# Convolutional FFN of a two-layer model: weight scales by exponent shifts out of PSUM, and one pool of four raw weight tiles

## The chip, the cores and the metric

The kernel runs on one core of a Trainium2 chip. The metric is the device time of one execution in microseconds (us). TensorE does matrix products into PSUM; VectorE, ScalarE and GpSimd do elementwise work, GpSimd only in SBUF; SyncE issues the transfers (DMAs) in one in-order queue.

## The reference

A model of two layers, 1024 tokens, width 1024, in float32. Layer 0 has a hybrid attention, layer 1 a latent attention (neither is touched here); after each comes the same kind of FFN:

```python
def conv_ffn(h, w_up, conv_w, conv_b, w_down):      # FFN_DIM = 2816, CONV_WIDTH = 3
    u = h @ w_up                                     # 1024 -> 2 * 2816
    u = causal_depthwise_conv(u, conv_w) + conv_b    # 3 taps along the tokens, per channel
    g, val = jnp.split(u, 2, axis=-1)
    return (jax.nn.silu(g) * val) @ w_down           # 2816 -> 1024

for i in range(2):
    x = x + mixer_i(rms_norm(x, attn_norm[i]))
    x = x + conv_ffn(rms_norm(x, ffn_norm[i]), ffn_w_up[i], ffn_conv_w[i], ffn_conv_b[i], ffn_w_down[i])
return rms_norm(x, final_norm)
```

## The kernel before

Every product is done in split precision: an operand is a high and a low 16-bit float (`up_h`, `up_l`; `dn_h`, `dn_l`; `qah`, `qal`), and three products of the halves are added in PSUM. So that the halves fit the range of the 16-bit format, each weight tile and each group of activations is first multiplied by a power of two, and the result is later multiplied by its inverse. Finding these powers of two is what the change is about.

**Stages of one FFN.** `mixer_out` (line 786) opens the pools, finds the scale of the norm's gain (`sh`, inverse `ish`), prepares the first two up weight tiles and runs the second half of the attention's output projection (`op.second`), after each block of which the block is normalised (`norm_xn`) and turned into seven blocks for a Strassen-like product (`block_turn`). `ffn_body` (line 812) then loops over j = 0..21. `ffn_up(j)` multiplies 12 x 7 times with the weights of tile j (`product`, line 561), evacuates the products into `u` (`keep` on ScalarE, line 567; `plus` on VectorE, line 571), asks for the weights of tile j + 2 (`up_weights`), and does the convolution (lines 603 to 606), SiLU, gating (line 610) and a Square that sums the squares of the gated values (line 611). Some j also ask for the down weights of a pair of tiles (`down_weights`, 11 in one FFN). When a group of one or two pairs is complete, `ffn_down` finds the group's scale (`down_scale`) and multiplies (line 722), adding into `x` (line 728) on VectorE.

**One up weight tile** (`up_weights`, line 461): two loads of 512 KB into two raw tiles (tag `up_raw`, two buffers, so one set); a Square of each on ScalarE that also gives the sums per partition, `ss` (line 470); VectorE adds the two sums into `sb` (line 473); TensorE multiplies with a matrix of ones, which spreads the sum over all partitions (line 476); VectorE scales it out of PSUM into `t` (line 478). `power` (line 451) then takes t to the power -1/2 on GpSimd (line 455), masks the mantissa away on VectorE, which gives the scale `s` (line 336), and three more VectorE instructions give the inverse `u` (reciprocal, times 1.25, mask). VectorE multiplies the tile's convolution weights `cw` by `u` and `ish` (line 483). GpSimd makes three sums of the raw tiles (lines 495 to 500), and ScalarE and VectorE or GpSimd split them (lines 636 to 640). **One down tile** (`down_weights`, line 642) goes the same way, with its own set of two raw tiles (tag `dn_raw`, which the gain and every other normalised block use too) and one more product on GpSimd, `uu` (line 664). `down_scale` (line 689) adds the sums of squares of a group, spreads them, takes the larger of its pairs (line 699) and calls `power`.

**Order.** Nothing is ordered by hand. A planner orders each engine's instructions when the program is built, from estimated durations, the order in which the code asks for them and the raised priorities (`tc.high_priority`); a buffer of a tag is given to the next tile when its last reader is done. On the chip each engine and the load queue then run strictly in that order, so an instruction that waits holds up all that stand behind it.

Of the kernel before, what the change touches and what calls it, by code (L numbers as in the profile page):

```python
# [21 lines left out]
P = 128  # L22
S = 1024
D = 1024
# [22 lines left out]
def model_kernel(ctx: ExitStack, tc: tile.TileContext, a: dict, out: bass.AP, dbg: dict):  # L47
# [58 lines left out]
    nc.gpsimd.memset(ones_sq, 1.0)  # L106
# [354 lines left out]
    def up_weights(li, j, up, cw, ish):  # L461
# [4 lines left out]
        ss = up.tile([P, 2], F32, name="wss", tag="wss", bufs=2)  # L466
        for q in range(2):
            raw.append(up.tile([P, 4, 256], F32, name="up_raw", tag="up_raw", bufs=2))
            load = nc.sync.dma_start(out=raw[q], in_=a["w_up"][li, j, :, q * 4:q * 4 + 4, :])
            nc.scalar.activation(out=sums.rearrange("p k t c -> p k (t c)"), in_=raw[q],  # L470
                                 func=AF.Square, accum_out=ss[:, q:q + 1])
# [79 lines left out]
    def ffn_up(li, j, up, dns, pairs, blocks, cw, weights, ish):  # L551
# [45 lines left out]
        if j + 2 < NF:  # L597
            weights.append(up_weights(li, j + 2, up, cw, ish))
# [12 lines left out]
        nc.scalar.activation(out=gate, in_=val, func=AF.Square, accum_out=pair["ss"][:, h:h + 1])  # L611
# [11 lines left out]
    def new_pair(q, dns):  # L623
        dn = dns[q % 2]
        g = [g for g in GROUPS if q in g][0]
        if q == g[0]:
            grp[0] = {"ss": dns[0].tile([P, len(g), 2], F32, name="gss", tag="gss", bufs=2),
                      "u": dns[0].tile([P, len(g), 1], F32, name="dnu", tag="dnu", bufs=2),
                      "uu": dns[0].tile([P, len(g), 1], F32, name="duu", tag="duu", bufs=2)}
        group = grp[0]  # L630
        return {"g": dn.tile([P, 2, S], F32, name="g", tag="g", bufs=1 + q % 2), "dn": dn, "q": q,
                **{k: group[k][:, g.index(q)] for k in ("ss", "u", "uu")}, "group": group}
# [9 lines left out]
    def down_weights(li, up, pair, weights):  # L642
# [3 lines left out]
        for j in (2 * q, 2 * q + 1):  # L646
            raw.append(up.tile([P, D], F32, name="dn_raw", tag="dn_raw", bufs=2))
            nc.sync.dma_start(out=raw[-1], in_=a["ffn_w_down"][li, j * P:(j + 1) * P, :])
        sums = up.tile([P, 2, 512], F32, name="dn_s", tag="up_s", bufs=SB)
        ss = up.tile([P, 2], F32, name="dss", tag="wss", bufs=2)  # L650
        for i in range(2):
            nc.scalar.activation(out=sums.rearrange("p a c -> p (a c)"), in_=raw[i], func=AF.Square,
                                 accum_out=ss[:, i:i + 1])
        sb = up.tile([P, 2], BF16, name="dsb", tag="wsb", bufs=2)
        nc.vector.tensor_tensor(out=sb, in0=ss[:, 0:1].broadcast_to([P, 2]),
                                in1=ss[:, 1:2].broadcast_to([P, 2]), op=ALU.add)
        st = bank("sb", 1)
        nc.tensor.matmul(st[:, :2], ones_sq, sb, start=True, stop=True)
        t = up.tile([P, 1], F32, name="dt", tag="wt", bufs=2)
        nc.vector.tensor_scalar(out=t, in0=st[:, :1], scalar1=1.05 * 2.0 ** -28, scalar2=1e-30,  # L660
                                op0=ALU.mult, op1=ALU.max)
# [27 lines left out]
    def down_scale(ps_, dn, bank_=None):  # L689
# [3 lines left out]
        with tc.high_priority(TP):  # L693
# [928 lines left out]
```

## Time and profile before

| what | value |
|---|---|
| median of 3 runs | 2531.49 us (2531.34 to 2533.38) |
| the profiled execution | 2533.1 us, of which the span from first to last instruction is 2531.3 |
| busy in the span: TensorE / VectorE / ScalarE / GpSimd | 2286.3 / 2013.6 / 1516.3 / 1251.4 us |
| mean granted TensorE clock | 0.966 |
| first FFN body | about 627 to 1300 us |
| second FFN body | about 1830 to 2506 us |

The trace has one row for each instruction; views group them. In the rows below PE is TensorE, PEld its weight loads, DVE VectorE, ACT ScalarE, POOL GpSimd, SPq the load queue; L473 is line 473 of the kernel; `out<-in` are the names of tiles. "A <- B: total, times, longest" means that engine and line A stood idle until B was done. A busy TensorE is not TensorE at its peak, as matmuls overlap.

### The profile page before, as it was taken

What the parts mean: (1) busy time and instruction counts of PE and PEld (TensorE: products, weight loads), DVE (VectorE), ACT (ScalarE), POOL (GpSimd) and SP (SyncE); (2) the same over time, 40 slices, a digit from 0 to 9 for tenths busy, and PEclk for the clock granted to TensorE, in tenths of its full rate; (3) what the DMA queues carried; (4) which work ended last, traced back from release to release, by engine and by line L of the source; (5) the groups of instructions that cost most, each with busy time, mean ns of one, the idle gap of its engine ahead of it and who ended that gap; (6) DMA issues with size and microseconds to landing.
All of it is one profiled execution on the core that took longest, in us unless ns stands there. A gap on an engine that the chain in (4) does not pass through costs nothing. (4 is left out here: it accounts for less than half of the span.)

```text
span 2531.3 us, 32238 instructions
## 1 busy us (share of the span) xinstructions
PE 2286.3 (90%) x10960; PEld 1358.3 (54%) x10960; DVE 2013.6 (80%) x3577; ACT 1516.3 (60%) x2533; POOL 1251.4 (49%) x1312
## 2 busy tenths in 40 slices
PE   8999999998889989898999877878898998989898
PEld 7877778676333434343448665556643343434343
DVE  6777887768787887887886887885878788788787
ACT  5676666536665555656545777773666556555653
POOL 4444433206465564656316777640746556465631
PEclk9999999899999999999999898989899999999999
DMA  4466633661111111111131787899121111111111
GB/s 134 101 138 121 127 77 80 201 178 61 61 55 50 45 56 50 50 42 59 34 112 32 141 169 150 161 257 242 51 63 52 49 48 53 50 50 42 59 42 67
DMA packets 324549, 228.46 MB, mean 90 GB/s; under 512 B 280288, under 2 KB 283360, under 8 KB 323936
## 3 DMA queue, kind: packets, MB, share of 16 engines
q1 hardware_dynamic: 324384, 226.40, 34.9%
q8 instruction: 86, 1.41, 0.2%
q14 instruction: 79, 0.65, 0.1%
HBM read 127.79 MB, written 25.43 MB: 61 GB/s over the span
## 5 line engine op out<-in xcount | busy, mean ns | idle before, releaser
L561 PEld LDWEIGHTS <-up_h 128*128 128x128 f16 x2464 | 241.6, 99 | 364.2 <-issue 73.8
L264 ACT ACTIVATE prob<-prob,m 128x512 f32<-128x512 f32 (+7 forms) x256 | 198.5, 776 | 103.7 <-DVE m L261 81.5
L289 DVE SCALAR_TENSOR_TENSOR hl<-prob,rl,hl 128x128 f16<-128x128 f32 (+6 forms) x196 | 199.0, 1027 | 25.5 <-ACT hl L288 24.6
L561 PEld LDWEIGHTS <-up_l 128*128 128x128 f16 x1232 | 122.2, 99 | 170.6 <-DVE up_l L640 21.7
L125 PE MATMUL bank_t<-hw_h,hTh 128*128 128x384 f32 x512 | 186.1, 366 | 2.8 <-DVE hTl L110 1.6
L126 PE MATMUL bank_t<-hw_l,hTh 128*128 128x384 f32 x512 | 176.9, 345 | 1.7 <-DVE hw_l L110 1.7
L288 ACT ACTIVATE hl<-prob,rl 128x128 f16<-128x128 f32 (+6 forms) x196 | 149.0, 778 | 47.6 <-DVE prob L1025 17.1
L127 PE MATMUL bank_t<-hw_h,hTl 128*128 128x384 f32 x512 | 175.4, 343 | 0.4 <-DVE hTl L110 0.4
L252 PE MATMUL wide<-k,q 96*128 96x512 f32 (+7 forms) x576 | 142.1, 388 | 37.1 <-DVE m L261 28.8
L261 DVE CUSTOM_DVE_ANT_0 prob<-wide,maskc 128x256 f32<-128x256 f32 (+3 forms) x192 | 143.9, 751 | 36.0 <-PE wide L252 32.9
L722 PEld LDWEIGHTS <-qah 128*128 128x128 f16 x896 | 86.3, 98 | 115.1 <-issue 10.7
L470 ACT ACTIVATE up_s<-up_raw 128x1024 f32<-128x1024 f32 x88 | 92.7, 1053 | 88.8 <-DMA up_raw<-in_w_up_dram 70.1
L728 DVE SCALAR_TENSOR_TENSOR x<-bank_a,gun,x 128x512 f32<-128x512 f32 x168 | 123.2, 743 | 19.3 <-PE bank_a L722 17.9
L252 PEld LDWEIGHTS wide<-k,q 128*128 128x128 f32 (+1 forms) x576 | 106.5, 214 | 57.1 <-DVE m L261 34.9
L500 POOL TENSOR_TENSOR up_raw<-up_raw,up_s 128x512 f32<-128x512 f32 x44 | 81.3, 1848 | 100.4 <-DVE up_l L640 69.0
L495 POOL TENSOR_TENSOR up_s<-up_raw 128x512 f32<-128x512 f32 x44 | 59.1, 1343 | 134.5 <-ACT up_s L470 128.3
L640 DVE SCALAR_TENSOR_TENSOR up_l<-up_raw,wsc,up_h 128x1024 f16<-128x1024 f32 x84 | 119.1, 1426 | 0.9 <-ACT up_h L639 0.7
L728 DVE SCALAR_TENSOR_TENSOR x<-bank_b,gun,x 128x512 f32<-128x512 f32 x152 | 112.5, 742 | 7.3 <-PE bank_b L722 7.1
L639 ACT ACTIVATE up_h<-up_raw,wsc 128x1024 f16<-128x1024 f32 x84 | 92.2, 1141 | 42.6 <-DVE wsc L336 42.5
L329 PEld LDWEIGHTS <-V 128*128 128x128 f16 x840 | 74.6, 100 | 73.6 <-issue 28.5
L110 POOL TENSOR_TENSOR up_l<-up_raw,up_h 128x512 f16<-128x512 f32 (+1 forms) x48 | 72.9, 1518 | 74.3 <-ACT up_h L117 44.3
L125 PEld LDWEIGHTS bank_t<-hw_h,hTh 128*128 128x128 f32 x512 | 97.5, 191 | 19.1 <-issue 12.3
(457 smaller groups left out, 7425.5 us busy)
## 6 DMA issues: line engine op xcount, KB each, us to landing
up_raw<-in_w_up_dram SPq DMA_DIRECT2D x88, 512.0 KB, 3.8
dn_raw<-in_ffn_w_down_dram SPq DMA_DIRECT2D x44, 512.0 KB, 3.7
hw_raw<-in_w_hyb_dram SPq DMA_DIRECT2D x32, 384.0 KB, 3.7
OTa<-ohl SPq DMA_DIRECT2D x16, 512.0 KB, 2.9
oa<-OTa SPq DMA_DIRECT2D x16, 512.0 KB, 6.2
OTb<-ohl SPq DMA_DIRECT2D x16, 512.0 KB, 3.8
xb<-in_x_dram SPq DMA_DIRECT2D x8, 512.0 KB, 5.7
x<-in_x_dram SPq DMA_DIRECT2D x8, 512.0 KB, 7.2
```

Source lines behind the costliest of these rows:

```text
L125: nc.tensor.matmul(out_, sh, mh, start=start, stop=False)
L126: nc.tensor.matmul(out_, sh, ml, start=False, stop=False)
L127: nc.tensor.matmul(out_, sl, mh, start=False, stop=stop)
L252: nc.tensor.matmul(sp[:, h * 512:h * 512 + w], q[:, qs], k[:, c:c + w], start=n == 0, stop=n == len(passes) - 1)
L261: nc.vector.tensor_tensor_reduce(out=pv, in0=sv, in1=mv, scale=-scale, scalar=3e38, op0=ALU.add, op1=ALU.min, accum_out=m)
L264: nc.scalar.activation(out=pv, in_=pv, func=AF.Exp, bias=m, scale=-1.0, accum_out=l)
L288: nc.scalar.activation(out=hi, in_=v, func=AF.Copy, scale=r)
L289: nc.vector.scalar_tensor_tensor(out=lo, in0=v, scalar=r, in1=hi, op0=ALU.mult, op1=ALU.subtract)
L470: nc.scalar.activation(out=sums.rearrange("p k t c -> p k (t c)"), in_=raw[q], func=AF.Square, accum_out=ss[:, q:q + 1])
L561: nc.tensor.matmul(o, w[side][p][:, k], blocks[block][q][:, k], start=first and k == n == 0, stop=k == 3 and n == 2, skip_group_check=not ...
L640: nc.vector.scalar_tensor_tensor(out=l, in0=x, scalar=s, in1=h, op0=ALU.mult, op1=ALU.subtract)
L728: nc.vector.scalar_tensor_tensor(out=x_, in0=m, scalar=un, in1=x_, op0=ALU.mult, op1=ALU.add)
```

## The change

The scale is no longer a power -1/2 with a masked mantissa: the exponent of the sum is halved by shifts and subtracted from a constant, as integers. The constant factor that `t` had goes into the matrix of ones, whose entries become 1.0625 x 2^-28. The sums of halves go: the Square writes its sums as bfloat16, and TensorE adds the two columns itself, as two matmuls into the same place. The inverse `u` is one integer addition, and VectorE's product of the convolution weights becomes a ScalarE Copy with scale `u`, while `ish` is multiplied into all of them at once on GpSimd. `down_scale` finds its scale in the same way, and `uu` goes. Raw tiles of up and down weights, the gain and every other normalised block share one tag, `raw`, of four buffers. The second up tile is asked for after the output projection's second half.

```diff
-    nc.gpsimd.memset(ones_sq, 1.0)
+    nc.gpsimd.memset(ones_sq, 1.0625 * 2.0 ** -28)
...
+    def halved(x, t):
+        nc.vector.tensor_scalar(out=x, in0=t.bitcast(I32), scalar1=24, scalar2=23,
+                                op0=ALU.logical_shift_right, op1=ALU.logical_shift_left)
+
     def power(s, u, t, pool):
-        v = pool.tile([P, 1], F32, name="pw", tag="pw", bufs=2)
+        x = pool.tile([P, 1], I32, name="pw", tag="pw", bufs=2)
         with tc.high_priority(TP):
-            nc.gpsimd.tensor_tensor(out=v, in0=t, in1=neghalf[:, :1], op=ALU.pow)
-            pow2(s, v)
-        nc.vector.reciprocal(out=v, in_=s)
-        nc.vector.tensor_scalar(out=v, in0=v, scalar1=1.25, scalar2=None, op0=ALU.mult)
-        pow2(u, v)
+            halved(x, t)
+            nc.vector.tensor_scalar(out=s.bitcast(I32), in0=x, scalar1=-1, scalar2=189 << 23,
+                                    op0=ALU.mult, op1=ALU.add)
+        nc.vector.tensor_scalar(out=u.bitcast(I32), in0=x, scalar1=65 << 23, scalar2=None, op0=ALU.add)
+
+    def over_partitions(st, sums):
+        for n, c in enumerate(sums):
+            nc.tensor.matmul(st, ones_sq, c, start=n == 0, stop=n == len(sums) - 1)
...
-        ss = up.tile([P, 2], F32, name="wss", tag="wss", bufs=2)
+        ss = up.tile([P, 2], BF16, name="wss", tag="wss", bufs=2)
...
-            raw.append(up.tile([P, 4, 256], F32, name="up_raw", tag="up_raw", bufs=2))
+            raw.append(up.tile([P, 4, 256], F32, name="up_raw", tag="raw", bufs=4))
...
-        sb = up.tile([P, 2], BF16, name="wsb", tag="wsb", bufs=2)
-        nc.vector.tensor_tensor(out=sb, in0=ss[:, 0:1].broadcast_to([P, 2]),
-                                in1=ss[:, 1:2].broadcast_to([P, 2]), op=ALU.add)
         st = bank("sb", 1)
-        nc.tensor.matmul(st[:, :2], ones_sq, sb, start=True, stop=True)
-        t = up.tile([P, 1], F32, name="wt", tag="wt", bufs=2)
-        nc.vector.tensor_scalar(out=t, in0=st[:, :1], scalar1=1.05 * 2.0 ** -28, scalar2=1e-30,
-                                op0=ALU.mult, op1=ALU.max)
+        over_partitions(st[:, :2], [ss[:, q:q + 1].broadcast_to([P, 2]) for q in range(2)])
...
-        power(s, u, t, up)
-        nc.vector.tensor_scalar(out=cw[:, j, :, 0:3], in0=cw[:, j, :, 0:3], scalar1=u, scalar2=ish,
-                                op0=ALU.mult, op1=ALU.mult)
+        power(s, u, st[:, :1], up)
+        nc.scalar.activation(out=cw[:, j, :, 0:3], in_=cw[:, j, :, 0:3], func=AF.Copy, scale=u)
...
-        power(s, pair["u"], t, up)
-        nc.gpsimd.tensor_scalar(out=pair["uu"], in0=pair["u"], scalar1=pair["u"], scalar2=1.05 * 2.0 ** -28,
-                                op0=ALU.mult, op1=ALU.mult)
+        power(s, pair["u"], st[:, :1], up)
...
-            sb = dn.tile([P, np_], BF16, name="gsb", tag="gsb", bufs=2)
-            nc.vector.tensor_tensor(out=sb, in0=ss[:, :, 0], in1=ss[:, :, 1], op=ALU.add)
-            st = (bank_ or bank_b)()
-            nc.tensor.matmul(st[:, :np_], ones_sq, sb, start=True, stop=True)
-            y, t = (dn.tile([P, n], F32, name=f"gy{n}", tag=f"gy{n}", bufs=2) for n in (2, 1))
-            nc.vector.tensor_tensor_reduce(out=y[:, :np_], in0=st[:, :np_], in1=grp_["uu"][:, :, 0], scale=1.0,
-                                           scalar=1e-30, op0=ALU.mult, op1=ALU.max, accum_out=t)
...
-        power(tau, un, t, dn)
...
+            over_partitions(st[:, :2], ss)
+            halved(r.bitcast(I32), st[:, :np_])
+            nc.vector.tensor_scalar(out=r.bitcast(I32), in0=r.bitcast(I32), scalar1=65 << 23, scalar2=None, op0=ALU.add)
+            nc.vector.tensor_scalar(out=un, in0=r[:, 0:1], scalar1=gu[:, 0:1], scalar2=None, op0=ALU.mult)
+            if np_ == 2:
+                nc.vector.tensor_scalar(out=un, in0=r[:, 1:2], scalar1=gu[:, 1:2], scalar2=un, op0=ALU.mult, op1=ALU.max)
+            nc.vector.tensor_scalar(out=tau.bitcast(I32), in0=un.bitcast(I32), scalar1=-1, scalar2=254 << 23,
+                                    op0=ALU.mult, op1=ALU.add)
             nc.vector.tensor_scalar(out=sg, in0=gu, scalar1=tau, scalar2=None, op0=ALU.mult)
...
-        gain = load_gain(up, f"ffn_norm{li}", D, "dn_raw", 2)
+        gain = load_gain(up, f"ffn_norm{li}", D, "raw", 4)
...
-        weights = [up_weights(li, j, up, cw, ish) for j in range(2)]
+        nc.gpsimd.tensor_scalar(out=cw[:, :, :, 0:3], in0=cw[:, :, :, 0:3], scalar1=ish, scalar2=1.0,
+                                op0=ALU.mult, op1=ALU.mult)
+        weights = [up_weights(li, 0, up, cw)]
...
-            xn = norm_xn(up, op.x[b], gain, *(("acc", AB), ("dn_raw", 2))[SO.index(b) % 2])
+            xn = norm_xn(up, op.x[b], gain, *(("acc", AB), ("raw", 4))[SO.index(b) % 2])
...
         op.second(nxt)
+        weights.append(up_weights(li, 1, up, cw))
```

## Rows read from the trace of the kernel before

**Rows 1.** Stages (length; busy PE, PEld, DVE, ACT, POOL): step, first body, both.

```profile
561.00:620.00 59.00, 55.41 (x249) 43.00 (x247) 45.74 (x70) 32.56 (x53) 35.48 (x33) 0.97 0.29 99
...
627.00:1300.00 673.00, 612.92 (x2766) 268.70 (x2763) 547.34 (x776) 391.00 (x555) 347.06 (x318) 0.98 0.16 51
...
sum 1349.00, PE 1231.62 PEld 539.38 DVE 1095.95 ACT 782.49 POOL 694.00; mean PE 615.81 PEld 269.69 DVE 547.98 ACT 391.24 POOL 347.00
```

**Rows 2.** TensorE's waits in the first FFN body (us in total, times, longest).

```profile
PE prod L561 <- ACT u L567: 11.1, 8, 3.2
PE prod L561 <- ACT up_h L639: 8.2, 6, 4.2
PE prod L561 <- DVE u L571: 6.8, 8, 3.3
PE bank_b L722 <- DVE x L728: 6.8, 9, 1.8
PE prod L561 <- DVE up_l L640: 6.6, 5, 2.4
PE sb L476 <- DVE wsb L473: 3.7, 5, 1.0
PE bank_b L697 <- DVE gsb L695: 3.4, 3, 2.2
...
PE sb L658 <- DVE wt L478: 2.2, 1, 2.2
```

**Rows 3.** Waits of all engines over the whole span.

```profile
ACT up_s L470 <- DMA up_raw<-in_w_up_dram: 70.1, 37, 5.9
...
ACT up_h L639 <- DVE wsc L336: 42.5, 20, 3.6
```

**Rows 4.** Groups of VectorE, whole span: busy us, mean ns, idle us before.

```profile
L640 DVE SCALAR_TENSOR_TENSOR up_l<-up_raw,wsc,up_h 128x1024 f16<-128x1024 f32 x84 | 119.1, 1426 | 0.9 <-ACT up_h L639 0.7
...
L483 DVE TENSOR_SCALAR convw<-convw,wun,hun 128x6 f32<-128x6 f32 x44 | 27.2, 618 | 0.5
...
L473 DVE TENSOR_TENSOR wsb<-wss 128x2 bf16<-128x2 f32 x44 | 18.8, 426 | 36.6 <-ACT up_s L470 36.5
...
L458 DVE TENSOR_SCALAR pw<-pw 128x1 f32<-128x1 f32 x82 | 12.2, 148 | 1.2
...
L336 DVE TENSOR_SCALAR wsc<-pw 128x1 int32<-128x1 int32 x44 | 6.6, 149 | 16.4 <-POOL pw L455 16.2
L478 DVE TENSOR_SCALAR wt<-sb 128x1 f32<-128x1 f32 x44 | 6.4, 146 | 0.0
...
L695 DVE TENSOR_TENSOR gsb<-gss 128x2 bf16<-128x2 f32 (+1 forms) x14 | 4.8, 344 | 5.5 <-ACT acc L611 5.5
```

**Rows 5.** Two tiles' instructions: duration ns as min/median/max, then first and last start.

```profile
L483 DVE TENSOR_SCALAR convw<-convw,wun,hun x44: 274/370/2118, 587.4 to 2449.0; 128x6 f32<-128x6 f32 x44
...
L336 DVE TENSOR_SCALAR wsc<-pw x44: 134/153/155, 581.7 to 2445.7; 128x1 int32<-128x1 int32 x44
```

**Rows 6.** Groups of GpSimd, whole span.

```profile
L455 POOL TENSOR_TENSOR pw<-wt,neghalf 128x1 f32<-128x1 f32 x44 | 43.5, 988 | 45.3 <-DVE wt L478 45.3
...
L664 POOL TENSOR_SCALAR duu<-dnu 128x1 f32<-128x1 f32 x22 | 13.3, 605 | 22.2 <-DVE dnu L336 17.9 <-ACT qah L639 3.7
...
L455 POOL TENSOR_TENSOR pw<-gy,neghalf 128x1 f32<-128x1 f32 x14 | 11.9, 848 | 90.5 <-DVE gy L699 90.5
```

**Rows 7.** Groups: small ScalarE instruction, sum matmul. Timeline: four sum matmuls in attention.

```profile
L969 ACT ACTIVATE lams<-lams 128x2 f32<-128x2 f32 x1 | 0.2, 191 | 0.0
...
L476 PE MATMUL sb<-wsb,ones_sq 128*128 128x2 bf16 x44 | 7.5, 171 | 10.5 <-DVE wsb L473 9.3 <-DVE dnu L336 1.2
...
66.92 0.25 PE L883 MATMUL bank_t<-g,wsq 128*128 128x2 bf16 x4
```

**Rows 8.** Timeline of VectorE, 1020 to 1024 us: start, us, instruction.

```profile
1020.96 0.15 DVE L478 TENSOR_SCALAR wt<-sb 128x1 f32<-128x1 f32 x1
...
1023.18 0.15 DVE L336 TENSOR_SCALAR wsc<-pw 128x1 int32<-128x1 int32 x1 [0.44 <-POOL pw L455]
```

More of the change, by code (lines that the diff above doesn't have):

```diff
@@ L464, in up_weights @@
+    def up_weights(li, j, up, cw):
         raw = []
         sums = up.tile([P, 4, 2, P], F32, name="up_s", tag="up_s", bufs=SB)
[L466 removed]
+        ss = up.tile([P, 2], BF16, name="wss", tag="wss", bufs=2)
         for q in range(2):
[L468 removed]
+            raw.append(up.tile([P, 4, 256], F32, name="up_raw", tag="raw", bufs=4))
             load = nc.sync.dma_start(out=raw[q], in_=a["w_up"][li, j, :, q * 4:q * 4 + 4, :])
[L470 to L471 removed]
@@ L472, in up_weights @@
-        sb = up.tile([P, 2], BF16, name="wsb", tag="wsb", bufs=2)
-        nc.vector.tensor_tensor(out=sb, in0=ss[:, 0:1].broadcast_to([P, 2]),
-                                in1=ss[:, 1:2].broadcast_to([P, 2]), op=ALU.add)
+            with nc.allow_low_precision("it chooses a power of two"):
+                nc.scalar.activation(out=sums.rearrange("p k t c -> p k (t c)"), in_=raw[q],
+                                     func=AF.Square, accum_out=ss[:, q:q + 1])
         st = bank("sb", 1)
-        nc.tensor.matmul(st[:, :2], ones_sq, sb, start=True, stop=True)
@@ L549, in block_turn, with ffn_up @@
         put(blocks, "t4", tok, t4)
-    def ffn_up(li, j, up, dns, pairs, blocks, cw, weights, ish):
+    def ffn_up(li, j, up, dns, pairs, blocks, cw, weights):
         w, _ = weights.pop(0)
@@ L597, in ffn_up @@
         if j + 2 < NF:
-            weights.append(up_weights(li, j + 2, up, cw, ish))
+            weights.append(up_weights(li, j + 2, up, cw))
         gate = up.tile([P, S], F32, name="acc", tag="acc", bufs=AB)
@@ L610, in ffn_up @@
         nc.vector.tensor_tensor(out=val, in0=gate, in1=val, op=ALU.mult)
-        nc.scalar.activation(out=gate, in_=val, func=AF.Square, accum_out=pair["ss"][:, h:h + 1])
+        with nc.allow_low_precision("it chooses a power of two"):
+            nc.scalar.activation(out=gate, in_=val, func=AF.Square, accum_out=pair["ss"][:, h:h + 1])
     GROUPS = ((0,), (1, 2), (3, 4), (5, 6), (7, 8), (9,), (10,))
@@ L626, in new_pair @@
         if q == g[0]:
-            grp[0] = {"ss": dns[0].tile([P, len(g), 2], F32, name="gss", tag="gss", bufs=2),
-                      "u": dns[0].tile([P, len(g), 1], F32, name="dnu", tag="dnu", bufs=2),
-                      "uu": dns[0].tile([P, len(g), 1], F32, name="duu", tag="duu", bufs=2)}
+            grp[0] = {"ss": dns[0].tile([P, len(g), 2], BF16, name="gss", tag="gss", bufs=2),
+                      "u": dns[0].tile([P, len(g), 1], F32, name="dnu", tag="dnu", bufs=2)}
         group = grp[0]
         return {"g": dn.tile([P, 2, S], F32, name="g", tag="g", bufs=1 + q % 2), "dn": dn, "q": q,
-                **{k: group[k][:, g.index(q)] for k in ("ss", "u", "uu")}, "group": group}
+                **{k: group[k][:, g.index(q)] for k in ("ss", "u")}, "group": group}
     def scaled_split(h, l, x, s, by_pool=False):
@@ L646, in down_weights @@
         for j in (2 * q, 2 * q + 1):
-            raw.append(up.tile([P, D], F32, name="dn_raw", tag="dn_raw", bufs=2))
+            raw.append(up.tile([P, D], F32, name="dn_raw", tag="raw", bufs=4))
             nc.sync.dma_start(out=raw[-1], in_=a["ffn_w_down"][li, j * P:(j + 1) * P, :])
         sums = up.tile([P, 2, 512], F32, name="dn_s", tag="up_s", bufs=SB)
[L650 to L656, printed above, removed]
+        ss = up.tile([P, 2], BF16, name="dss", tag="wss", bufs=2)
+        with nc.allow_low_precision("it chooses a power of two"):
+            for i in range(2):
+                nc.scalar.activation(out=sums.rearrange("p a c -> p (a c)"), in_=raw[i], func=AF.Square,
+                                     accum_out=ss[:, i:i + 1])
         st = bank("sb", 1)
[L658 to L661, printed above, removed]
+        over_partitions(st[:, :2], [ss[:, i:i + 1].broadcast_to([P, 2]) for i in range(2)])
         s = up.tile([P, 1], F32, name="dsc", tag="wsc", bufs=2)
-        power(s, pair["u"], t, up)
-        nc.gpsimd.tensor_scalar(out=pair["uu"], in0=pair["u"], scalar1=pair["u"], scalar2=1.05 * 2.0 ** -28,
-                                op0=ALU.mult, op1=ALU.mult)
+        power(s, pair["u"], st[:, :1], up)
         (b11, b12), (b21, b22) = (halves(v) for v in raw)
@@ L816, in ffn_body @@
         for j in range(NF):
-            ffn_up(li, j, up, dns, pairs, blocks, cw, weights, ish)
+            ffn_up(li, j, up, dns, pairs, blocks, cw, weights)
             if len(groups) > 2 and j == 2 * groups[0][-1] + 1:
```

12 lines of the change are left out of this document (8 added, 4 removed).

## The prediction

> **What bounds the kernel now.** I read the page first, then the table by stage, then the waits of TensorE within one FFN, then the groups of VectorE and GpSimd, and last single tiles. The edits touch the two FFN halves and the step that leads into each. In the table by stage [rows 1] the two FFN bodies take 1349 of the span's 2531.3 us. In them TensorE is busy 1231.6, so it stands idle 117.4 us; VectorE is busy 1096 (81%), ScalarE 782 (58%), GpSimd 694 (51%). TensorE is the bound, and VectorE is the engine that it most often waits for or that holds up whoever it waits for. [...]
>
> TensorE's waits in the first body [rows 2] fall in two kinds. Waits that end with a weight tile or with the sum that sets its scale: up_h 8.2, up_l 6.6, wsb 3.7, gsb 3.4, wt 2.2, together 24.1 us. Waits for the evacuation of products, u from ScalarE 11.1, u from VectorE 6.8, x 6.8, together 24.7. The second body is the same program, and I double these: 48 and 49 us (the rest of the 117.4 is in smaller rows).
>
> The first kind hangs on a chain: the load, two Squares on ScalarE, VectorE's wsb, TensorE's sum, VectorE's wt, GpSimd's power, VectorE's wsc, and only then the splits. ScalarE stood idle 42.5 us for wsc and 70.1 us for the load of a raw tile [rows 3], since with one set of two raw tiles for the up weights a load can only start when the last split of the tile before is done.
>
> **VectorE's work.** Removed [rows 4]: the sums of halves, wsb 18.8, gsb 4.8 and the 22 dsb at wsb's mean of 0.43, 9.4: 33.0; 66 scalings out of PSUM (wt and dt) at 0.146 = 9.6; 82 reciprocals and 82 multiplies at 0.148 = 24.3; 164 maskings at 0.149 = 24.4; convw 27.2; the 14 reductions of the groups at 0.15 = 2.1. That is 121 us. Added: for 68 scales (66 weight tiles, 2 gains) three instructions each, and for the 14 groups four, with a fifth in the 8 groups of two pairs: 204 + 64 = 268, none of which the trace shows in this form. The nearest rows are one-element integer instructions at 0.149; the upper bound is convw's mean, 0.618. I take 0.149, since shape and type are those of the masking: 40 us. Net VectorE loses 81 us, 40 in each half, 7% of its 1096 busy us there.
>
> The row that could speak against 0.149 is convw's [rows 5]: 128x6 elements took 0.37 us in the median and up to 2.12, while the masking, 128x1 and also out of SBUF, never took more than 0.155. [...]
>
> The first new instruction reads PSUM. [...] The rows have 0.146 out of PSUM (wt) and 0.149 out of SBUF (wsc) [rows 4], and these decide.
>
> **GpSimd's work.** Removed [rows 6]: 82 powers, 43.5 us for the 44 up tiles, 11.9 for the 14 groups, and for the 22 down tiles and two gains 24 at the groups' mean of 0.85, 20.4; and duu, 13.3: 89 us of 694. Added: one multiply over all convolution weights in each half, at twice duu's mean of 0.6 under 3 us, on an engine that is half idle. GpSimd also stood 90.5 us with a group's power at the head of its queue, waiting for gy; what is queued behind it (the g_s subtractions, the next weights' subtractions) may now go first.
>
> **ScalarE and TensorE.** 44 small Copies for convw go to ScalarE: nearest row 0.191 (128x2) [rows 7], 8.4 us in all, covered by an engine idle 42% of the time; with the cover gone it is 8.4. TensorE issues 160 sum matmuls instead of 80. Four of the same form in a row took 0.25 us against a mean of 0.171 for a single one [rows 7], so 0.03 for each further one: 2.4 us. If each cost its whole 0.171 it would be 13.7; I take 2.4, because the pipelined row has the same form, other weights each time.
>
> **The chain.** In the stretch of [rows 8] wt began at 1020.96 and wsc at 1023.18: 2.2 us for wt, the power with what was queued before it on GpSimd, and the hand-overs; the power alone has a mean of 0.99 [rows 6]. Afterwards two VectorE instructions follow each other, 0.3 us. With wsb's mean of 0.43 [rows 4] the chain is shorter by 1.1 to 2.3 us per tile. The sum matmul now waits for ScalarE alone, so wsb is no longer late in VectorE's queue.
>
> **The raw tiles.** Two sets of two become a pool of four for up and down weights, gain and half of the normalised blocks. Where two up tiles follow each other the second may load while the first is in use: the load's wait of up to 5.9 us leaves the chain. Where down tiles stand in between, a set may be held by them; then it is as before. The load queue is in order, so a load that waits for a slot holds up those behind it.
>
> **The step into the FFN.** The second up tile moves behind the output projection's second half. Between 561 and 620 us VectorE is busy 45.7 of 59 [rows 1]; the tile's wsb, convw and first split, 0.4 + 0.6 + 1.4 us, and its small ones leave that stretch. I take 2 us off each half; above, 5, below, nothing, since the tile must be ready one product stage later and could be late there.
>
> **The sum** is made against the profiled execution, 2533.1 us with 1.8 around the span; the median of the runs is 1.6 below it. Weight and scale waits, 48 us: the chain gets shorter by as much as a typical wait (up_h's 8.2 in 6 times is 1.4), but the planner will move the instructions anew, so I take half, -24; bounds 0 and -48. Evacuation waits, 49 us: VectorE's queue gets 7% shorter, in a stage where it is 81% full; I take a quarter, -12; bounds 0 and -33 (81 less 48). Clock: 0.98 over 1349 us is 27 us lost to the lower level; less than a third of the idle time goes, and I take a fifth, -5; bounds 0 and -9. The step into the FFN -4, bounds 0 and -10. TensorE +2, bound +14; ScalarE 0, bound +8. Together -43: 2490 against the profiled time, **2489** as a median. The bounds add up to about +22 and -100; but no more than the 81 us of VectorE is a sensible floor, about 2450.
>
> **Rivals.** *VectorE is the bound.* It is the fullest engine behind TensorE, and nearly every wait passes it. If all its saved time comes back, 81 us: 2450. Against it: TensorE's own 1232 us leave only 117, of which 81 would be two thirds.
>
> *The chain was hidden.* TensorE has products of other tiles and of the down stage to run while a scale is late; its waits for u and x stay where they are because the planner fills VectorE's holes with splits again. Then only half the sum's waits go (wsb, gsb, wt: 9.3 a half), less the matmuls: -5 to -8, 2525. For it: ScalarE's 42.5 us for wsc is no TensorE time.
>
> *ScalarE's queue is held by u (the slower one).* Before, convw was VectorE's own and ScalarE waited for nothing there. Now a Copy on ScalarE waits for the low-priority instruction that makes u on VectorE; behind it in ScalarE's queue stand the copies of the products, for which TensorE already waits 11.1 us a half. If one split of VectorE (1.43 us, up_l's mean [rows 4]) stands before u for each of the 44 tiles, that is 63 us. It decides from 43 / 44 = 1.0 us a tile; at 1.43 the result is +20: 2551.
>
> *The new small instructions are drawn out by GpSimd* as convw was, two of three at 0.62: some 178 x 0.47 = 84 us, and VectorE gains nothing; GpSimd's removal and the pool still give the half of the weight waits: -20, 2511. Against it stands the 0.155.
>
> **Chances.** Forecast 0.58, by itself 2465 to 2512; VectorE the bound 0.10; hidden 0.12; ScalarE held 0.15; drawn out 0.05. A measurement of this kernel can tell about 0.2%, 5 us. The hidden case divides into 0.08 within that and 0.04 faster; so faster 0.77, same 0.08, slower 0.15. The range is 2450 to 2535: it takes in all but the far part of the slower case and the lower half of the VectorE case.
>
> **What would show it.** Right: no power among GpSimd's groups and its busy time down by some 85 us; VectorE down by about 80; integer instructions of 0.15 us; the sum matmuls waiting for ScalarE; up_h and up_l gone from TensorE's waits or halved; ScalarE's waits for loads (70.1) much shorter; FFN bodies of about 655 us. Wrong: convw's Copy on ScalarE with long waits for VectorE and TensorE's wait for u above 11 a half; new VectorE instructions of 0.4 us or more; loads that wait for down tiles; up tile 1 late at the second product stage; VectorE's busy time down and TensorE's idle time unchanged.

## The result and the profile after

The changed kernel takes 2467.5 us (2466.4 to 2468.4), the one before in the same comparison 2532.4 (2531.3 to 2533.9): a ratio of 0.974, 95% interval 0.973 to 0.976, 65 us less. The forecast was 2489, so the sign and the range were right and the gain was half as large again as forecast (65 against 43). The profiled execution took 2466.8 us with a span of 2464.7, 66.6 less than before.

Cut into stages at the first product of an FFN's up tiles (line 564, before 561) and its last down product (723, before 722), the span changes like this (us, from the timelines of TensorE):

| stage | before | after | change |
|---|---|---|---|
| up to the first FFN's products | 627.9 | 623.6 | -4.3 |
| first FFN body | 713.7 | 685.2 | -28.5 |
| second layer's attention and step | 489.0 | 489.6 | +0.6 |
| second FFN body | 691.3 | 657.0 | -34.3 |
| after it | 9.4 | 9.3 | -0.1 |

The gain lies in the two bodies. The stages ahead of them can be divided at the last product of the attention's weights with V (line 329); all edits but the value in the matrix of ones come behind it. Counted from there the steps into the FFN took 82.5 and 79.6 us before and 80.5 and 74.0 after. The attention parts, which hold no edit, took 545.4 and 409.4 before and 543.1 and 415.6 after.

Busy time of the engines over the whole span (first part of the page after: us, share of the span, instructions):

```profile
PE 2267.4 (92%) x11040; PEld 1360.5 (55%) x11040; DVE 1967.5 (80%) x3299; ACT 1523.0 (62%) x2577; POOL 1164.3 (47%) x1210
```

GpSimd had 1251.4 before and VectorE 2013.6: 87 and 46 less. The same in the two bodies (view by stretches of the kernel after; busy PE, PEld, VectorE, ScalarE, GpSimd, then the granted clock):

```profile
623.60:1308.80 685.20, 646.40 (x3000) 296.48 (x2999) 562.98 (x711) 421.18 (x630) 328.28 (x304) 0.97 0.18 60
1798.40:2455.40 657.00, 621.19 (x2891) 278.18 (x2888) 547.19 (x677) 408.14 (x599) 319.54 (x283) 0.99 0.17 54
sum 1342.20, PE 1267.59 PEld 574.66 DVE 1110.17 ACT 829.32 POOL 647.82; mean PE 633.79 PEld 287.33 DVE 555.09 ACT 414.66 POOL 323.91
```

The two stretches of the kernel before, in the same view:

```profile
sum 1405.00, PE 1285.90 PEld 571.18 DVE 1144.11 ACT 811.43 POOL 710.11; mean PE 642.95 PEld 285.59 DVE 572.06 ACT 405.72 POOL 355.05
```

[rows 1] has somewhat shorter windows, which leave out the bodies' ends. So TensorE's idle time falls from 119.1 to 74.6, by 44.5, and its busy time by 18.3 although it issues 80 matmuls more. What it still waits for in the first body (us in total, times, longest; the waits of the kernel after):

```profile
PE prod L564 <- DVE u L574: 9.1, 7, 2.9
PE prod L564 <- ACT up_h L642: 6.3, 3, 2.1
PE sb L468 <- DVE pw L453: 3.8, 1, 3.8
PE bank_a L723 <- DVE x L729: 3.6, 4, 1.3
...
PE sb L468 <- ACT up_s L480: 2.3, 3, 1.1
...
PE prod L564 <- ACT u L570: 1.6, 4, 0.5
...
PE bank_b L723 <- DVE x L729: 1.3, 1, 1.3
PE bank_b L468 <- ACT acc L615: 0.8, 1, 0.8
```

Against [rows 2]: weight tiles and sums 24.1 there, 13.2 here (up_h 6.3, sb 3.8 and 2.3, bank_b from acc 0.8); up_l is gone, and so are wsb, gsb and wt, which no longer exist. Evacuations 24.7 there, 15.6 here; u from ScalarE fell from 11.1 to 1.6.

The waits of the other engines in the whole span of the kernel after, beside [rows 3]:

```profile
DVE up_l L643 <- ACT up_h L642: 64.5, 33, 6.2
...
ACT up_s L480 <- DMA up_raw<-in_w_up_dram: 42.4, 22, 5.3
```

ScalarE's wait for the loads of the up weights is down from 70.1 to 42.4, and its wait for wsc from 42.5 to 11.9. VectorE's wait for up_h has come in their place, 64.5 against 6.4 before: it now stands ready before ScalarE has made the high half. The row of before, in the same view:

```profile
DVE up_l L640 <- ACT up_h L639: 6.4, 8, 1.6
```

The new instructions, and the largest group of the old ones (VectorE's groups of the kernel after: busy us, mean ns, idle us before, as in [rows 4]):

```profile
L643 DVE SCALAR_TENSOR_TENSOR up_l<-up_raw,wsc,up_h 128x1024 f16<-128x1024 f32 x84 | 129.6, 1549 | 59.8 <-ACT up_h L642 55.0 <-POOL g L751 4.8
...
L453 DVE TENSOR_SCALAR pw<-sb 128x1 int32<-128x1 int32 x66 | 9.7, 146 | 0.1
L461 DVE TENSOR_SCALAR wsc<-pw 128x1 int32<-128x1 int32 x44 | 6.5, 148 | 0.7
L463 DVE TENSOR_SCALAR wun<-pw 128x1 int32<-128x1 int32 x44 | 6.2, 142 | 0.0
```

They take what the masking took, and VectorE stands idle before them for less than 1 us in all; before, it stood 36.6 us at wsb and 16.4 at wsc [rows 4]. The chain that took 2.2 us from wt to wsc [rows 8] is now this (VectorE's timeline of the kernel after: start, us, instruction):

```profile
1017.66 0.14 DVE L453 TENSOR_SCALAR pw<-sb 128x1 int32<-128x1 int32 x1
1017.84 0.15 DVE L461 TENSOR_SCALAR wsc<-pw 128x1 int32<-128x1 int32 x1
1017.90 0.14 DVE L463 TENSOR_SCALAR wun<-pw 128x1 int32<-128x1 int32 x1
```

0.18 us from pw to wsc. ScalarE's small product of the convolution weights (ScalarE's groups of the kernel after) took 12.6 us, where 8.4 was forecast, and waited 1.2 us in all:

```profile
L487 ACT ACTIVATE convw<-convw,wun 128x6 f32<-128x6 f32 x44 | 12.6, 286 | 1.2 <-DVE wun L463 1.2
```

### The profile page after: what moved, and what is told of

It reads as the page before. It is cut to its first block, busy times and chain, and to the rows that moved or that the text cites. A ratio compares the mean times of both kernels' runs of the same rounds, so it can differ in the third digit from the quotient of the medians.

```text
span 2464.7 us, 32161 instructions
## 1 busy us (share of the span) xinstructions
PE 2267.4 (92%) x11040; PEld 1360.5 (55%) x11040; DVE 1967.5 (80%) x3299; ACT 1523.0 (62%) x2577; POOL 1164.3 (47%) x1210
## 5 line engine op out<-in xcount | busy, mean ns | idle before, releaser
L289 DVE SCALAR_TENSOR_TENSOR hl<-prob,rl,hl 128x896 f16<-128x896 f32 (+6 forms) x196 | 196.1, 1013 | 30.9 <-ACT hl L288 30.3
L288 ACT ACTIVATE hl<-prob,rl 128x896 f16<-128x896 f32 (+6 forms) x196 | 148.7, 777 | 51.2 <-DVE prob L1029 17.2
L643 DVE SCALAR_TENSOR_TENSOR up_l<-up_raw,wsc,up_h 128x1024 f16<-128x1024 f32 x84 | 129.6, 1549 | 59.8 <-ACT up_h L642 55.0
L729 DVE SCALAR_TENSOR_TENSOR x<-bank_a,gun,x 128x512 f32<-128x512 f32 x168 | 123.2, 743 | 24.4 <-PE bank_a L723 22.3
L480 ACT ACTIVATE up_s<-up_raw 128x1024 f32<-128x1024 f32 x88 | 92.6, 1053 | 70.8 <-DMA up_raw<-in_w_up_dram 42.4
L729 DVE SCALAR_TENSOR_TENSOR x<-bank_b,gun,x 128x512 f32<-128x512 f32 x152 | 112.1, 743 | 28.5 <-PE bank_b L723 28.3
L570 ACT COPY u<-prod 128x512 f32<-128x512 f32 x176 | 99.5, 571 | 40.6 <-PE prod L564 31.4
L503 POOL TENSOR_TENSOR up_raw<-up_raw,up_s 128x512 f32<-128x512 f32 x44 | 73.9, 1680 | 97.3 <-DVE up_l L643 66.4
L574 DVE TENSOR_TENSOR u<-prod,u 128x512 f32<-128x512 f32 x132 | 89.3, 681 | 26.9 <-ACT u L570 16.4
```

The costliest lines, as they stand in the source:

```text
L288: nc.scalar.activation(out=hi, in_=v, func=AF.Copy, scale=r)
L289: nc.vector.scalar_tensor_tensor(out=lo, in0=v, scalar=r, in1=hi, op0=ALU.mult, op1=ALU.subtract)
L643: nc.vector.scalar_tensor_tensor(out=l, in0=x, scalar=s, in1=h, op0=ALU.mult, op1=ALU.subtract)
L729: nc.vector.scalar_tensor_tensor(out=x_, in0=m, scalar=un, in1=x_, op0=ALU.mult, op1=ALU.add)
```

## The experiments

Three theories of the gain were to be told apart. *Chain*: the way from load to scale was late for TensorE, and each microsecond out of it counts. *VectorE's work*: its queue got shorter, so splits and evacuations come earlier. *Pool*: the loads had been late. A fourth thing came up on the way: an instruction that waits at the head of VectorE's queue holds back the work behind it. In the kernel before VectorE stood idle 1.85 us until wsb began at 1040.46 us; the acc of line 606 behind it, whose only wait, for the acc of line 604, had ended at 1038.63, began at 1040.54. I call its idle time that ended with an instruction that finds a scale (wsb, dsb, gsb, wsc, dsc, gtau and their successors) its *head waits*, and took it from VectorE's waits over the whole span. It is a chosen part of VectorE's idle time: its waits at other instructions, such as the 64.5 us at up_l above, are not in it, nor is a tile of the first attention that is also called wsc. All waits of VectorE in the two bodies together were 254 us before and 225 after.

All results in one table. Bodies: length of the two FFN bodies together and VectorE's busy time in them. The last two columns are TensorE's waits in both bodies, the rows of the waits added by what ended them: weight tiles and sums; u and x. In 23 places the view names a small VectorE instruction (py, pg, pw, wsc, wun or dnu) although up_l, u or x ended 0.05 us ahead of TensorE's start; these waits are counted with up_l, u and x. "Saved" is what the median's ratio to the kernel before in the same comparison falls short of 1, times 2531. Each kernel has one trace; the columns behind "saved" come from it.

| kernel | us | ratio (95% interval) | saved | bodies | VectorE | head waits | weights, sums | u and x |
|---|---|---|---|---|---|---|---|---|
| before | 2532.4 | 1 | 0 | 1405.0 | 1144 | 109 | 52 | 51 |
| changed | 2467.5 | 0.974 (0.973 to 0.976) | 65 | 1342.2 | 1110 | 0 | 26 | 33 |
| e1_pool | 2486.5 | 0.983 (0.982 to 0.985) | 42 | 1356.6 | 1151 | 79 | 26 | 41 |
| e1b_pool_order | 2476.8 | 0.980 (0.977 to 0.984) | 51 | 1362.3 | 1153 | 92 | 28 | 46 |
| e2_scales | 2480.3 | 0.981 (0.979 to 0.983) | 48 | 1356.6 | 1093 | 33 | 29 | 40 |
| e3_order | 2521.8 | 0.997 (0.996 to 0.998) | 8 | 1391.0 | 1139 | 101 | 47 | 49 |
| e8_load | 2472.3 | 0.976 (0.975 to 0.978) | 60 | 1348.4 | 1147 | 1 | 24 | 29 |
| e9_chain | 2451.0 | 0.967 (0.966 to 0.969) | 83 | 1331.3 | 1095 | 49 | 18 | 35 |
| e7_pow | 2488.6 | 0.982 (0.981 to 0.984) | 45 | 1357.2 | 1122 | 55 | 22 | 42 |
| e6_sums_dve | 2471.6 | 0.978 (0.976 to 0.979) | 57 | 1352.5 | 1130 | 38 | 25 | 41 |
| e10_group | 2479.2 | 0.981 (0.979 to 0.982) | 49 | 1358.7 | 1108 | 18 | 20 | 37 |
| e5_conv_dve | 2451.4 | 0.968 (0.966 to 0.970) | 81 | 1335.5 | 1129 | 2 | 17 | 28 |
| n3_conv_late | 2459.5 | 0.973 (0.971 to 0.974) | 70 | 1341.9 | 1110 | 0 | 27 | 30 |
| n4_conv_late_before | 2528.8 | 0.999 (0.998 to 1.000) | 3 | 1399.6 | 1144 | 105 | 47 | 49 |

One thing must be seen before the rows are compared. The stage between the bodies runs from 481.3 us (e5_conv_dve, e9_chain) to 496.3 (e7_pow). Its end, the step into the second FFN, holds edits. The attention ahead of that step holds none in any of these kernels, and yet it alone runs from 406.2 us (e6_sums_dve) to 422.0 (e7_pow): the planner lays out all instructions anew for each kernel. So a difference of some 15 us between two totals can come from a stage that nothing was done to; the column of the bodies leaves that out. The bodies scatter as well: e3_order has 14 us less in them though it edits only the step before them, n4_conv_late_before 5. A part of such differences can be chance between executions, since the kernel before alone took from 2525.2 to 2537.2 us over all comparisons.

**The parts of the change, each alone.** e1_pool is the kernel before with the four shared raw buffers only:

```diff
-            raw.append(up.tile([P, 4, 256], F32, name="up_raw", tag="up_raw", bufs=2))
+            raw.append(up.tile([P, 4, 256], F32, name="up_raw", tag="raw", bufs=4))
...
-            raw.append(up.tile([P, D], F32, name="dn_raw", tag="dn_raw", bufs=2))
+            raw.append(up.tile([P, D], F32, name="dn_raw", tag="raw", bufs=4))
...
```

> The kernel before with one change: up tiles, down tiles, gain and every other normalised block share one tag of four raw buffers; scales, GpSimd's power and the order of the second up tile stay as before. Theory A (the scale chain and VectorE's load carry the gain, the pool a small part): -5 to -20 us against before. Rival P (the pool carries it, because loads no longer wait for the tile before): -40 us or more. Rival N (the planner's new order carries it, whatever the edit): anything between +15 and -40, unrelated to the waits for loads.

e3_order is the kernel before with the second up tile asked for later, and e1b_pool_order has both edits:

```diff
-        weights = [up_weights(li, j, up, cw, ish) for j in range(2)]
+        weights = [up_weights(li, 0, up, cw, ish)]
...
         op.second(nxt)
+        weights.append(up_weights(li, 1, up, cw, ish))
```

> The kernel before with the second up tile alone moved behind the output projection's second half. Theory A: -4 us (0 to -10), all in the step into the FFN, bodies unchanged within 3 us. Rival N: the bodies move too, by 5 us or more, though no work in them changed; that would size the planner's own scatter.

> The kernel before with the pool of four and with the second up tile asked for after the output projection's second half. Theory A: -8 to -25 us against before, 2 to 8 us of it in the step into the FFN. Rival P: -45 us or more. Rival N: no regular relation to the run with the pool alone.

e2_scales is the changed kernel with two sets of two raw tiles and the old order, so it has the new scales only (the diff is that of e1_pool and e3_order turned round).

> The changed kernel with two sets of two raw tiles and with both first up tiles asked for ahead of the projection's second half, as before; so the scales, sums and convw alone. Theory A: -35 to -55 us against before (the larger part of the 65). Rival P: -20 us or less. Rival N: no relation.

The pool alone gives 42 us, the new scales alone 48, the order 8; together 65, not 98. The parts draw on the same idle time. With the pool ScalarE's wait for the up loads falls from 70.1 [rows 3] to 39.9 us (ScalarE's waits in e1_pool):

```profile
ACT up_s L470 <- DMA up_raw<-in_w_up_dram: 39.9, 27, 4.6
```

Then VectorE's sums of halves are late less often, although they are still there (VectorE's waits in e1_pool):

```profile
DVE wsc L336 <- POOL pw L455: 32.0, 30, 3.0
...
DVE dsb L655 <- ACT dn_s L652: 15.8, 7, 4.0
...
DVE wsb L473 <- ACT up_s L470: 9.3, 12, 2.7
```

Before, wsb stood at the head of the queue for 36.5 us and dsb for 28.0. The new scales take these two instructions away altogether; in e2_scales VectorE's first look at the sum is what waits instead (VectorE's waits there), behind loads that are as late as before (73.4 us):

```profile
DVE pw L453 <- PE sb L468: 28.8, 14, 4.1
```

Only with both parts do the head waits vanish. e1b_pool_order settles nothing between the pool alone and all: its runs spread from 2469.6 to 2489.5, and its profiled execution is at the upper end.

Against what was expected: the pool's 42 us are rival P's (40 or more), not theory A's 5 to 20, and the 48 of the scales alone lie in theory A's 35 to 55. The 51 of e1b_pool_order fit rival P (45 or more). The 8 us of e3_order lie in theory A's 0 to 10, but not where it had them. Counted from the last product with V, its steps took 82.5 and 84.1 us, against 82.5 and 79.6 before; its bodies moved by 14, as rival N had it.

**VectorE's work.** e8_load adds eight one-element instructions to each of the 68 scales of the changed kernel; their result isn't used:

```diff
+        y = pool.tile([P, 1], F32, name="py", tag="py", bufs=2)
+        for _ in range(8):
+            nc.vector.tensor_scalar(out=y.bitcast(I32), in0=x, scalar1=65 << 23, scalar2=None, op0=ALU.add)
```

> The changed kernel with eight more one-element VectorE instructions for each of its 68 scales, behind u, which nothing waits for: VectorE +80 us (544 x 0.147), the chain and all else as in the changed kernel. Theory A (VectorE's load is what counts, and it sits at 83% of the FFN bodies): +30 to +60 us against the changed kernel. Rival C (the chain counts, the load does not): under +15.

The work was there (VectorE's groups in e8_load):

```profile
L466 DVE TENSOR_SCALAR py<-pw 128x1 int32<-128x1 int32 x544 | 79.2, 147 | 8.2
```

It nearly equals the 81 us that the change takes off VectorE, and costs 5 us, with ratios whose intervals overlap: rival C's price, not theory A's 30 to 60. VectorE's busy time in the bodies rises by 37 us only, since other instructions took less time here (last section); that makes it as busy there as before the change (1147 us against 1144), and yet the bodies are 57 us shorter than before (the two bodies of e8_load):

```profile
sum 1348.40, PE 1275.00 PEld 574.96 DVE 1146.70 ACT 833.48 POOL 660.12; mean PE 637.50 PEld 287.48 DVE 573.35 ACT 416.74 POOL 330.06
```

TensorE's waits for u and x did not grow: 29 us against the changed kernel's 33, four waits for u that bear py's name included (TensorE's waits in the first body of e8_load):

```profile
PE prod L567 <- ACT u L573: 6.8, 8, 3.1
...
PE prod L567 <- DVE u L577: 3.8, 5, 2.9
...
PE prod L567 <- DVE py L466: 1.9, 2, 1.4
PE bank_b L726 <- DVE x L732: 1.8, 1, 1.8
```

e1_pool says the same from the other side: VectorE's busy time rose by 7 us, and TensorE's waits for u and x fell by 10. So VectorE's amount of work is not what bounded the bodies.

**The chain.** e9_chain puts one GpSimd instruction, a multiplication by one, into each scale's chain of the changed kernel:

```diff
...
-            halved(x, t)
+            halved(x0, t)
+            nc.gpsimd.tensor_tensor(out=x.bitcast(F32), in0=x0.bitcast(F32), in1=ones[:, :1], op=ALU.mult)
```

> The changed kernel with one GpSimd multiply by 1 between the halved exponent and the scale of all 68 scales: the chain is as long as with the power (1 to 2 us more a tile), GpSimd +50 us, VectorE unchanged. Rival C (the chain counts): +12 to +25 us against the changed kernel. Theory A's load part: under +8. Together with the run with more VectorE load this parts chain from load.

e7_pow has the old power and VectorE's five instructions in the place of the three, for tiles and gains but not for the groups:

```diff
...
-            halved(x, t)
-            nc.vector.tensor_scalar(out=s.bitcast(I32), in0=x, scalar1=-1, scalar2=189 << 23,
-                                    op0=ALU.mult, op1=ALU.add)
-        nc.vector.tensor_scalar(out=u.bitcast(I32), in0=x, scalar1=65 << 23, scalar2=None, op0=ALU.add)
+            nc.vector.tensor_scalar(out=t1, in0=t, scalar1=1.0, scalar2=1e-30, op0=ALU.mult, op1=ALU.max)
+            nc.gpsimd.tensor_tensor(out=v, in0=t1, in1=neghalf[:, :1], op=ALU.pow)
+            pow2(s, v)
+        nc.vector.reciprocal(out=v, in_=s)
+        nc.vector.tensor_scalar(out=v, in0=v, scalar1=1.25, scalar2=None, op0=ALU.mult)
+        pow2(u, v)
```

> The changed kernel with GpSimd's power and VectorE's five instructions of each up, down and gain scale again; sums by two matmuls, groups by exponents, pool of four and order as in the changed kernel. Theory A: the chain longer by 1 to 2.3 us a tile, VectorE +20 us, GpSimd +62: +15 to +30 us against the changed kernel. Rival F (with the pool of four a late scale is no longer late for TensorE): within +-8.

The chain got longer in both (GpSimd's groups in e9_chain, then VectorE's waits there):

```profile
L462 POOL TENSOR_TENSOR pw<-pw,ones 128x1 f32<-128x1 f32 x68 | 36.1, 531 | 67.7 <-DVE pw L453 67.7
```

```profile
DVE wsc L463 <- POOL pw L462: 41.1, 29, 3.5
```

With it VectorE stood 41.1 us at wsc again, and yet e9_chain is 17 us faster than the changed kernel (in the profiled executions 11 in the bodies, 8 in the attention between them). Rival C had it 12 to 25 us slower; theory A's "under +8" is met, but nothing in that theory makes it faster. e7_pow, with 39.3 us at wsc and a power of 0.85 us in the mean, is 21 slower (15 in the bodies), inside theory A's 15 to 30. Half a microsecond more per chain is thus not what decides, and the chain theory in its simple form falls. TensorE's waits for weights and sums do not come back either: 18 us in e9_chain and 22 in e7_pow, against 26. What sets the two apart stays open.

e6_sums_dve gives the tiles their sums of halves on VectorE back, e10_group the groups their whole old scale (sum, uu, power):

```diff
-        over_partitions(st[:, :2], [ss[:, q:q + 1].broadcast_to([P, 2]) for q in range(2)])
+        sb = up.tile([P, 2], BF16, name="wsb", tag="wsb", bufs=2)
+        nc.vector.tensor_tensor(out=sb, in0=ss[:, 0:1].broadcast_to([P, 2]),
+                                in1=ss[:, 1:2].broadcast_to([P, 2]), op=ALU.add)
+        over_partitions(st[:, :2], [sb])
...
```

> The changed kernel with VectorE's sums of halves again for up and down tiles (a sum in float32, one matmul); scales by exponents, pool of four and order as changed. TensorE's sum matmul waits for VectorE again. Theory Q (TensorE's in-order queue, held at the sum matmul by a late VectorE, is what the scale part freed): +15 to +30 us against the changed kernel, and waits of TensorE at the sum of 10 us in each half. Theory N: within the scatter of the two runs above, without such waits.

```diff
+            sb = dn.tile([P, np_], BF16, name="gsb", tag="gsb", bufs=2)
+            nc.vector.tensor_tensor(out=sb, in0=ss[:, :, 0], in1=ss[:, :, 1], op=ALU.add)
...
+            nc.gpsimd.tensor_tensor(out=v, in0=t, in1=neghalf[:, :1], op=ALU.pow)
+            pow2(tau, v)
...
```

> The changed kernel with the group's scale found as before: VectorE's sum, one matmul, the product with uu, GpSimd's power and the inverse by VectorE (14 groups); tiles' scales, pool and order as changed. Theory Q: +5 to +15 us against the changed kernel, since TensorE waited 3.4 us a half at the group's sum and the down products start later. Theory N: within the scatter.

The sums cost 10 us in the bodies, and they bring back waits at the head of the queue (VectorE's waits in e6_sums_dve):

```profile
DVE dsb L663 <- ACT dn_s L659: 19.3, 14, 4.1
...
DVE wsb L484 <- ACT up_s L480: 12.9, 12, 2.9
```

TensorE's waits for u and x rise from 33 to 41 with them. The sums bring back 10 us of TensorE's waits at wsb in both bodies together, where theory Q had 10 in each, and the total is 4 to 8 us longer, not 15 to 30. The group's old scale costs 16.5 in the bodies; its head waits are only 18 us, and TensorE's waits for u and x rise to 37. In the total it costs 12 to 16, near theory Q's 5 to 15, but not by TensorE's waits at the group's sum: these are 0.4 us.

A rival that no run isolates is GpSimd's work, which the change cuts in the bodies from 710 to 648 us. e1_pool keeps all of it (710), and its bodies are 48 us shorter than before, so the larger part of the gain does not need the cut. But the two variants of the changed kernel that put most of it back, e7_pow (707) and e10_group (701), have the longest bodies of those with the pool, and the last 15 us could be GpSimd's.

**ScalarE's new work.** e5_conv_dve gives the product of the convolution weights back to VectorE; n3_conv_late leaves it on ScalarE and asks for it after the splits; n4_conv_late_before moves VectorE's product of the kernel before in the same way:

```diff
-        nc.scalar.activation(out=cw[:, j, :, 0:3], in_=cw[:, j, :, 0:3], func=AF.Copy, scale=u)
+        nc.vector.tensor_scalar(out=cw[:, j, :, 0:3], in0=cw[:, j, :, 0:3], scalar1=u, scalar2=1.0,
+                                op0=ALU.mult, op1=ALU.mult)
```

> The changed kernel with the convolution weights multiplied by u on VectorE again (ish stays on GpSimd). VectorE gets about 27 us back, ScalarE loses 12.6. Theory A (VectorE's load counts in full): +10 to +25 us against the changed kernel's 2467.5. Rival S (ScalarE held by u): no change or faster than the changed kernel. Rival F (both parts only fill one and the same pool of TensorE's idle time, some 75 us of which are left): within +-8.

```diff
-        nc.scalar.activation(out=cw[:, j, :, 0:3], in_=cw[:, j, :, 0:3], func=AF.Copy, scale=u)
...
         parts(3, r1[:, :, :1], "s4")
+        nc.scalar.activation(out=cw[:, j, :, 0:3], in_=cw[:, j, :, 0:3], func=AF.Copy, scale=u)
```

> The changed kernel with the same instructions; only the small Copy of the convolution weights is asked for after the tile's splits instead of ahead of them, so that the planner lays the queues out anew. Theory N (a new layout of the queues alone moves the time by 10 us or more, up or down): it differs from the changed kernel by 8 us or more, and so the single parts cannot be priced to better than that. Theory A (the time follows the work and the chain): within +-5 us of the changed kernel.

> The kernel before with the same instructions; only the product of the convolution weights is asked for after the tile's splits instead of ahead of them. Theory N: differs from before by 8 us or more either way. Theory A: within +-5 us, perhaps -5 to 0, as an instruction of 0.6 us stands later in VectorE's queue. If the kernel before were an unlucky layout, this run would be faster by 20 us or more.

On VectorE the product takes 25.9 us in place of ScalarE's 12.6 (VectorE's groups in e5_conv_dve):

```profile
L487 DVE TENSOR_SCALAR convw<-convw,wun 128x6 f32<-128x6 f32 x44 | 25.9, 589 | 0.8
```

The kernel is 16 us faster even so, 7 of them in the bodies and 8 in the attention between them. Theory A had it 10 to 25 slower. Rival S has the sign, but not its reason, since ScalarE waited 1.2 us at the Copy. Asking later leaves the bodies of the changed kernel as they were (-0.3 us), so the Copy's place in the order costs nothing there; the total is 5 to 8 us shorter, and the attention 6. n4_conv_late_before stays within theory A's 5 us. e5_conv_dve and e9_chain, both at 2451 us, are the fastest versions seen; that they give VectorE or GpSimd more work, and gain about as much in the attention as in the bodies, speaks for the layout, but no run shows it.

## Why the prediction was right, and where it was off

- **Weight and scale waits, -24: the size was right, the reason only in part.** Both bodies have 25.4 us of the rows that were forecast at 48 before (13.2 in the first, 12.2 in the second): -23. What the argument missed is that two causes fed them. It priced the chain and left the pool without a number, "the load's wait of up to 5.9 us leaves the chain"; each alone brings the group to 26 and 29 in the table's count, from 52, and both together to no less. With the pool in place a longer chain brought none of these waits back (e9_chain, e7_pow). "I take half" was a guess, and that it came out is partly luck.
- **Evacuation waits, -12: sized nearly right (-16, from 48.8 to 32.7), the reason refuted.** "VectorE's queue gets 7% shorter": e8_load makes it as busy as before, and the waits do not come back. What they go with is the head waits. Over the 14 kernels of the table a straight line through the two columns gives u and x = 31 us + 0.17 x head waits (correlation 0.94; 0.87 without before, e3_order and n4_conv_late_before, which are nearly one kernel). By it the 109 us that vanished are worth some 19 us of evacuation waits. This is an argument from columns that move together; no run changed the head waits and nothing else. It does not hold for the whole of the gain. For the length of the bodies the correlation is 0.81 with all 14 kernels and 0.53 without those three, and e9_chain, with 49 us of head waits, has the shortest bodies. Nor does every wait at the head of the queue count alike: the 64.5 us at up_l came in while the bodies got shorter.
- **Clock -5, TensorE +2: too small by 15.** Together -3 was forecast; TensorE's busy time fell by 18.3. The granted clock was 1.00 or 0.50 throughout both traces, with nothing between; the bodies had 62 us at 0.50 before and 48 after. The loss, added over the bodies in stretches of 5 us as (1 - granted clock) x length, fell from 30.9 to 24.1 us: -7 where -5 was forecast. That a fifth of it would go with the idle time was my estimate; no run isolates it. For the rest the waits give a clue: they number 122 before and 58 after, and a product's record is 0.38 us long where the next one starts 0.22 after it. By this estimate a gap that closes takes 0.16 us of busy time with it, 64 of them 10 us. That part belongs to the waits; the sum had no term for it.
- **The other small waits**, which had no term, gave about 6, the rest of TensorE's 44.5. Those for qal and qah fell from 11.9 to 4.4 us, while those for the transformed blocks rose from 2.2 to 7.5; the remainder is in smaller rows.
- **The step into the FFN, -4: agrees by luck.** The two stages that lead into a body changed by -4.3 and +0.6. Counted from the last product with V the steps gave 2.0 and 5.6, and the attention ahead of them moved by -2.3 and +6.2 without an edit. The order alone did not shorten the steps (e3_order).
- **VectorE -81: counted right, but it did not come back.** The removed groups had 123.2 us, the new ones have 41.5. VectorE's busy time fell by 46 all the same, since instructions that were not edited took 36 us more: up_l 129.6 against 119.1. The whole difference matters little, as e8_load shows.
- **GpSimd -86 (89 less 3): -87.** ScalarE's convw cost 12.6 in place of 8.4, under cover as forecast.
- **The rivals.** *VectorE is the bound* is refuted by e8_load: as much VectorE work as before, and 5 us more time than the changed kernel. *The chain was hidden* would have been 2525; the waits did go. *ScalarE held by u* did not come: 1.2 us of waits at the Copy and 1.6 for u in the first body. *Drawn out by GpSimd* did not come either: the longest pw, wsc or wun took 0.159 us, although 34 of the 44 wsc had a GpSimd instruction beside them. In the kernel before the 13 of the 44 convw that had none took 0.285 us in the mean, the other 31 took 0.757. In the groups' scale 22 one-element instructions on float32 (gun) took 0.20 to 0.27 in place of the 0.149 that was assumed, about 2 us in all.

Added up, -23, -16, -6, -18 and -4 are the 67 us by which the span fell. So the reason given to the evacuation term failed, and the terms that were too small are TensorE's own, the evacuations and the small waits that had none. All of them were off to the same side, which is why 43 became 65. A body is 31 us shorter in the mean; with 655 in place of 674 [rows 1] about 20 was written.

## What to carry to other kernels

The busy share of an engine with an in-order queue does not say what its work costs: here 79 us of small instructions put back into VectorE's queue cost 5. Look for the small instruction that stands at the head of the queue and waits for another engine, and either let the engine that needs the value compute it or make its input early; here the new scales alone gave 48 us and the earlier loads alone 42. That such waits are why TensorE waited less for its evacuations is likely, but not shown, and they do not price the whole gain. Two edits that remove the same waits don't add up. Where a planner lays out everything anew, compare stages that hold no edit first: here the attention moved by 16 us.

## What the runs showed of the hardware

- The same VectorE instructions take other times in another layout. The changed kernel and e2_scales have the same 3299 of them, and VectorE is busy 1967.5 and 1944.5 us; e9_chain has 1949.3 and e8_load 1918.7 without its 79.2. up_l, whose two operands are in SBUF, varies: its mean is 1549 ns in the changed kernel, 1443 in e8_load, 1552 in e9_chain. x and u, with one operand in PSUM, don't: x takes 743 to 744 in all three, u 681, 681 and 682. In the changed kernel the 26 of the 84 up_l that had no GpSimd instruction beside them took 1277 ns in the mean, the others 1671. For x the two means are 745 and 742, for u 682 and 681. No run isolates what about the instructions decides it.
- The one-element integer instructions of the scales were not drawn out: pw, wsc and wun stay between 0.135 and 0.159 us in the changed kernel, while the 128x6 product on VectorE went from 0.217 to 1.372 with a median of 0.404 (e5_conv_dve). One-element products on float32 that read a factor from a tile were longer, but as steady: gun with one such factor took 0.203 to 0.216, with two operands from tiles 0.260 to 0.269. No cost of reading PSUM shows at this size: pw out of PSUM took 146 ns in the mean, wsc out of SBUF 148.
- On GpSimd one element per partition took 0.85 us in the mean as a power (e7_pow) and 0.53 as a multiplication (e9_chain); the medians are 0.548 and 0.190, the longest 1.530 and 1.231.
